# Stick-breaking heads: additions to GpSimd, key copies to ScalarE, and the keys' lo over all 128 rows

## The chip, the core and the metric

The kernel runs on one core of a Trainium2 chip. The time is device microseconds of one execution, the median of several runs; the profiled execution is a further one. TensorE multiplies matrices, VectorE and ScalarE work element by element, GpSimd does so too but only on SBUF, and SyncE issues most of the loads.

## The reference, cut to what matters

Two blocks are applied to 512 tokens of width 1024, all in float32: a first one with a convolution layer and a pooling layer, a second one with stick-breaking attention, retention and a feed-forward part. The change touches the stick-breaking attention alone, 16 heads of width 64:

```
for i in range(s_len // BLOCK):            # BLOCK = 128, four query blocks
    end = (i + 1) * BLOCK
    z = einsum('bhtd,bhsd->bhts', qb, kb) * scale          # scale = 64 ** -0.5
    mask = s_pos[None, :] < t_pos[:, None]
    log_1m_beta = where(mask, log_sigmoid(-z), 0.0)
    after = cumsum(log_1m_beta, axis=3, reverse=True) - log_1m_beta
    log_a = log_sigmoid(z) + after
    a = where(mask, exp(log_a), 0.0)
    outs.append(einsum('bhts,bhsd->bhtd', a, vb))
```

With s = softplus(z) = -log_sigmoid(-z), log_a is z minus the sum of s over this key and all later ones, up to the query. So the kernel needs, for each head, the scores, their softplus, sums of it from the end, one exponential and the product with v.

## The kernel before

Every float32 operand of a matmul is split into a coarse part "hi" and the rest "lo" (both float32r), and a product is three matmuls: hi by hi, hi by lo, lo by hi. The weights come in 244 groups of 128x1024. For each group ScalarE casts the hi (L294) and VectorE subtracts for the lo (L299), two groups ahead of their use.

**Layout of a head.** Scores are kept transposed: keys on the 128 rows, queries on the columns. For key block j only queries from j*128 on count, so four blocks of 512, 384, 256 and 128 columns are laid into three PSUM banks, numbered n: bank 0 has block 0 (512 columns), bank 1 blocks 1 and 3 (384 + 128), bank 2 block 2 (256). They are worked through in the order 1, 2, 0. Tiles of banks 0 and 1 are named "s" (512 wide), those of bank 2 "u" (256 wide). PSUM: banks 0 and 1 come from four "z" buffers, bank 2 from two "r" buffers. Projections and head outputs take turns in two "m" buffers.

**Queries and keys.** A projection gives two heads, one on rows 0 to 63, one on 64 to 127. The tile of a query (`sb_q`) holds its hi on the rows of its head and its lo on the other 64 rows. For a key (`sb_k`) ScalarE takes the two hi from PSUM (L1065), VectorE subtracts both lo into the two halves of one tile (L1068), and VectorE copies each hi to the other 64 rows as well (L1070). So one 128-row matmul of the doubled key hi with the query tile gives hi by hi and hi by lo at once (L1097), and a 64-row matmul adds lo by hi (L1106).

**Softplus** (L1113 to L1127): VectorE takes the minimum with 40 (L1113), ScalarE an exponential (L1114) and a logarithm (L1115), VectorE a maximum with z (L1118). Then the softplus of later key blocks is added: block 2 takes block 3 (128 columns), block 1 takes block 2 (256), block 0 takes block 1 (384), all on VectorE (L1124). The sums are split: VectorE casts hi (L1080), GpSimd subtracts lo (L1081). Six matmuls with a triangle of -1 (L1135) and six with its complement (L1138) add the sums to the scores in PSUM, first with the three hi, then with the three lo. ScalarE takes the exponential (L1144); it is split in the same way (L1080 or L1078, then L1081), and eight matmuls with v (L1159) give the output in an "m" buffer. L1165 and L1167 put its two halves together.

**Order.** In this stage (`tc.manual_schedule`) ScalarE, GpSimd, VectorE and TensorE run their instructions in the order in which the program writes them. Each head is one step of six acts, STEP = "WOSFFF". In step h, W is `sb_weights` of head h (L1135, L1138, L1144), O is `sb_out` of head h-1 (L1159 to L1167), S is `sb_scores` of head h+2, and each F is the next piece of other work: half of a projection to q or k (12 matmuls of 512 columns), or a quarter of a v projection (24 of 256). F's come in a cycle of four steps: step 4 has q4 and the first half of k4, step 5 the second half of k4 and then q5, step 6 k5 and a quarter of v2, step 7 the rest of v2; the same holds for steps 0 to 3 and 8 to 11. From step 12 on there are four F's and they belong to the retention part.

The work of the other engines is written later than what it follows: after each act comes a `tick`, and a task that yields a number goes on after so many ticks, older tasks first. WAIT holds these numbers. With 2 for "min" and 1 for "max", the minimum of head h+2 is written after the first F of step h, the maximum and the first two additions after the second. With 2 for "split", the casts and subtractions of banks 2 and 1 of a head, the maximum and the addition of its bank 0 come after W of the step before its own, and the split of its bank 0 after S of that step. `finish` writes whatever is left of a task at once. The exponential of head h is split after S of step h (WAIT 3).

Of the kernel before, what the change touches and what calls it, by code (L numbers as in the profile page):

```python
# [9 lines left out]
F32 = mybir.dt.float32  # L10
F32R = mybir.dt.float32r
AF = mybir.ActivationFunctionType
ALU = mybir.AluOpType

P = 128
T = 512
# [51 lines left out]
).split()  # L68

WAIT = {"v": 1, "q": 1, "k": 1, "min": 2, "max": 1, "split": 2, "exp": 3, "out": 0}  # L70
START = "FFSFFFSFFF"
STEP = "WOSFFF"
ON = {"sp": "VVV", "aa": "AVA"}
# [60 lines left out]
def body(ctx: ExitStack, tc, ap, out):  # L134
# [12 lines left out]
    def nm(p):  # L147
        uid[0] += 1
        return f"{p}{uid[0]}"
# [16 lines left out]
    def at(tag="a", dt=F32, n=T):  # L166
        return phase[0].pool[tag].tile([P, n], dt, tag=tag, name=nm(tag))
# [4 lines left out]
    def pm():  # L172
        return psm.tile([P, T], F32, tag="m", name=nm("m"))

    def pz():
        return at("z")
# [4 lines left out]
    def pr():  # L181
        return psr.tile([P, T], F32, tag="r", name=nm("r"))

    def f(x):
        return x.bitcast(F32)

    mm = nc.tensor.matmul
    V, A, G = nc.vector, nc.scalar, nc.gpsimd

    HALF = (slice(0, 64), slice(64, 128))  # L190
# [6 lines left out]
    with tc.high_priority(offset=20000):  # L197
        for k in range(KC):
            t = const.tile([P, T], F32, name=nm("x"))
# [103 lines left out]
    def block(i, n=1):  # L303

        g, r = divmod(at_block[0] + i, GB)
        hi, lo = group(g)
        return hi[:, r * P:(r + n) * P], lo[:, r * P:(r + n) * P]

    def mm3(o, l, r, first, last):
        mm(o, l[0], r[0], start=first, stop=False)  # L310
        mm(o, l[0], r[1], start=False, stop=False)  # L311
        mm(o, l[1], r[0], start=False, stop=last)  # L312
# [505 lines left out]
    with tc.manual_schedule(engines=HAND):  # L818
# [7 lines left out]
        for k in range(KC):  # L826
            t = at("c")
# [63 lines left out]
    for i in range(4):  # L891
        t = at("v" if i < 2 else "p")
# [74 lines left out]
    n2 = Norm(lambda k: geff[:, 16 + k:17 + k], lambda k: mod[:, 48 + k:49 + k], "c")  # L967
# [17 lines left out]

    q_, k_, v_, osb = {}, {}, {}, []

    def lin_in(m):

        o = pm()  # L990
        for k in range(KC):
            mm3(o, block(0), h[k], k == 0, k == KC - 1)
            at_block[0] += 1
            if k == KC // 2 - 1:
                yield
        return o
# [33 lines left out]
    def post(work):  # L1030
        tasks.append([0, work])
        run(tasks[-1])
        return work
# [7 lines left out]
    def finish(work):  # L1041
        for t in list(tasks):
            while t[1] is work and t in tasks:
                run(t)

    def split_steps(o, t):
        A.copy(out=t[:, :, 0, :], in_=o)
        yield WAIT["v"]
        V.tensor_sub(out=t[:, :, 1, :], in0=o, in1=f(t[:, :, 0, :]))

    def sb_q(i, o):

        q_[i] = [at("a", F32R) for _ in HALF]
        for t, a in zip(q_[i], HALF):
            A.mul(out=t[a], in_=o[a], mul=0.125)
        yield WAIT["q"]
        for t, a, b in zip(q_[i], HALF, HALF[::-1]):
            V.scalar_tensor_tensor(out=t[b], in0=o[a], scalar=0.125, in1=f(t[a]), op0=ALU.mult, op1=ALU.subtract)

    def sb_k(i, o):  # L1060

        res, lo = [at("a", F32R) for _ in HALF], at("a", F32R)
        k_[i] = res, lo
        for t, a in zip(res, HALF):
            A.copy(out=t[a], in_=o[a])  # L1065
        yield WAIT["k"]
        for t, a in zip(res, HALF):
            V.tensor_sub(out=lo[a], in0=o[a], in1=f(t[a]))  # L1068
        for t, a, b in zip(res, HALF, HALF[::-1]):
            V.tensor_copy(out=t[b], in_=f(t[a]))  # L1070

    def sb_tile(n, dt=F32):
        return at("u", dt, T // 2) if n == 2 else at("s", dt)

    def sb_split(t, n, w, on):
        hi, lo = sb_tile(n, F32R), sb_tile(n, F32R)
        if on[n] == "A":
            A.copy(out=hi[:, 0:w], in_=t[:, 0:w])  # L1078
        else:
            V.tensor_copy(out=hi[:, 0:w], in_=t[:, 0:w])  # L1080
        G.tensor_tensor(out=lo[:, 0:w], in0=t[:, 0:w], in1=f(hi[:, 0:w]), op=ALU.subtract)  # L1081
        return hi, lo

    def sb_scores(hd):
        i, r = hd // 2, HALF[hd % 2]
        finish(ready.pop(f"q{i}", None))
        finish(ready.pop(f"k{i}", None))
        q, kh, kl = q_[i][hd % 2], k_[i][0][hd % 2], k_[i][1]
        zs, sp = {}, {}
        for n in (1, 2, 0):  # L1090
            bank = BANKS[n]
            z = pz() if n < 2 else pr()
            w = bank[-1][1] + bank[-1][2]
            zs[n] = z, w
        of_block = [(zs[n][0][:, off:off + wj], j, bi) for n in (1, 2, 0) for bi, (j, off, wj) in enumerate(BANKS[n])]
        for o, j, bi in of_block:
            mm(o, kh[:, j * P:j * P + P], q[:, j * P:T], start=bi == 0, stop=False, skip_group_check=True)  # L1097
        for n, (z, _) in zs.items():
            if len(BANKS[n]) == 2:
                m2 = z.rearrange("p (a b) -> p a b", a=4)[:, 0:4:3, :]  # L1100
                mm(m2, identr, mask.unsqueeze(1).to_broadcast([P, 2, P]), start=False, stop=False, skip_group_check=True)
            else:
                mm(z[:, 0:P], identr, mask, start=False, stop=False, skip_group_check=True)

        for o, j, bi in of_block:
            mm(o, kl[r, j * P:j * P + P], q[r, j * P:T], start=False, stop=True, skip_group_check=True)  # L1106

        def softplus():

            ts = {n: sb_tile(n) for n in zs}  # L1110
            yield WAIT["min"]
            for n, (z, w) in zs.items():
                V.tensor_scalar(out=ts[n][:, 0:w], in0=z[:, 0:w], scalar1=40.0, scalar2=None, op0=ALU.min)  # L1113
                A.activation(out=ts[n][:, 0:w], in_=ts[n][:, 0:w], func=AF.Exp)  # L1114
                A.activation(out=ts[n][:, 0:w], in_=ts[n][:, 0:w], func=AF.Ln, bias=1.0)  # L1115
            yield WAIT["max"]
            for n, (z, w) in zs.items():
                V.tensor_tensor(out=ts[n][:, 0:w], in0=z[:, 0:w], in1=ts[n][:, 0:w], op=ALU.max)  # L1118
                if n == 1:
                    continue  # L1120
                for j in (2, 1) if n == 2 else (0,):
                    (n1, o1, w1), (n2, o2, w2) = WHERE[j], WHERE[j + 1]
                    t1 = ts[n1][:, o1 + P:o1 + w1]
                    V.tensor_tensor(out=t1, in0=t1, in1=ts[n2][:, o2:o2 + w2], op=ALU.add)  # L1124
                yield WAIT["split"]
                for n1 in (2, 1) if n == 2 else (0,):
                    sp[n1] = sb_split(ts[n1], n1, zs[n1][1], ON["sp"])  # L1127

        return zs, sp, post(softplus())
# [127 lines left out]
    def lin_tok():  # L1257

        os = [pz() if j < 2 else pm() for j in range(4)]
        for k in range(KC):  # L1260
            wh, wl = block(0, 4)
            at_block[0] += 4
            for j, o in enumerate(os):
                hh, hl = cols(h[k], j * P, j * P + P)
                mm(o, hh, wh, start=k == 0, stop=False)  # L1265
                mm(o, hh, wl, start=False, stop=False)  # L1266
                mm(o, hl, wh, start=False, stop=k == KC - 1)  # L1267
        return [split(o) for o in os]
# [23 lines left out]
    def ret_out(sc, v, sg, meanwhile):  # L1292
        sq = Stat(G)
        oo = []
        for e in range(4):
            o = pz()
            for j in range(4):
                vl = cols(v[j], e * P, e * P + P)
                mm(o[:, j * P:T], vl[0], sc[j][0], start=j == 0, stop=False)
                mm(o[:, j * P:T], vl[0], sc[j][1], start=False, stop=False)  # L1300
                mm(o[:, j * P:T], vl[1], sc[j][0], start=False, stop=j == 3)
            oo.append(at("s"))
            V.tensor_tensor(out=oo[e], in0=o, in1=sg[e], op=ALU.mult)
            q2 = at("s")
            A.activation(out=q2, in_=o, func=AF.Square)  # L1305
            sq.add(q2)
        rb = pr()
        next(meanwhile)
        for i, _ in enumerate(rsqrt_steps(pr(), [sq.acc], 512, 0, T, rb)):
            if i == 1:  # L1310
                next(meanwhile)
        res = []
        for t in oo:
            V.tensor_tensor(out=t, in0=t, in1=rb, op=ALU.mult)
            hi, lo = at("a", F32R), at("a", F32R)
            A.copy(out=hi, in_=t)
            (G if len(res) % 2 else V).tensor_tensor(out=lo, in0=t, in1=f(hi), op=ALU.subtract)
            res.append((hi, lo))
        for _ in meanwhile:
            pass  # L1320
        return res
# [46 lines left out]
    for hd in range(RET_HEADS):  # L1368
        q, k_ = ret_in.pop(hd)
        if hd == 0:  # L1370
            osb = [split_in(osb[i], into=(at("o" if i else "s", F32R), at("s", F32R))) for i in range(KC)]
        v = lin_tok()
# [8 lines left out]
        res = ret_out(sc, v, sg, pairwise(ret_qk(hd + 1)) if hd < RET_HEADS - 1 else ret_branches())  # L1381
# [56 lines left out]
    with tc.manual_schedule(engines=HAND):  # L1438
# [5 lines left out]
        for a in (0, T // 2):  # L1444
            b = a + T // 2
            o = acc()
# [99 lines left out]
```

## Time and profile before

| | |
|---|---|
| median of 3 runs | 1676.9 us (1675.87 to 1680.08) |
| profiled execution | 1677.49 us, span 1675.7 us |
| TensorE busy | 1595.4 us (95%) |
| VectorE busy | 1015.4 us (61%) |
| ScalarE busy | 601.3 us (36%) |
| GpSimd busy | 498.4 us (30%) |
| granted TensorE clock, mean | 0.984 |

A matmul's duration in the trace overlaps that of the next, so TensorE's busy share is no measure of its speed. The stick-breaking stage runs from about 487 to 752 us of the span. A row of the timeline gives the start, the duration (of several instructions together where it ends in x2 or more), the engine (PE is TensorE, PEld its weight loads, DVE VectorE, ACT ScalarE, POOL GpSimd), the line, the tiles written and read, and in brackets how long the engine stood idle before and what ended that.

### The profile page before, as it was taken

The page shows a single profiled execution, that of the slowest core. Times are in us where ns is not written, and L with a number is a line of the kernel's source. Part 1 is how long each engine was busy: PE and PEld are TensorE (multiplying, and loading weights), DVE is VectorE, ACT ScalarE, POOL GpSimd, SP SyncE. Part 2 cuts the span into 40 slices and gives each one's busy share as a digit, 9 for nine tenths or more (in the row PEclk, how much of TensorE's full clock was granted, in tenths as well). Part 3 has the DMA queues.
Part 4 walks back from the last instruction along what each step waited for, and adds up shares of the span by engine and source line. Part 5 has one row for each costly group of instructions (what it writes and reads, how often), then busy time and mean ns, then how long its engine had stood idle before and what let it go on. Part 6 is the DMA issues. An engine that isn't in the chain of part 4 may idle for free.

```text
span 1675.7 us, 20285 instructions
## 1 busy us (share of the span) xinstructions
PE 1595.4 (95%) x7904; PEld 1345.8 (80%) x7904; DVE 1015.4 (61%) x1426; ACT 601.3 (36%) x896; POOL 498.4 (30%) x361
## 2 busy tenths in 40 slices
PE   6899899999989999999999999999999999999997
PEld 4688787877888888878878888888888888888887
DVE  6899978576678888886476644633254533333222
ACT  3434443433356566532332222223333522222221
POOL 2757854560124545550120201204431100000001
PEclk9999999899989999999999999999999999999999
DMA  7654544245621111215546232322232332332221
GB/s 253 200 187 158 178 139 145 89 146 183 223 75 52 56 59 51 76 64 172 170 149 210 96 115 66 104 88 76 90 99 76 101 100 91 99 101 93 96 91 61
DMA packets 59187, 195.91 MB, mean 117 GB/s; under 512 B 6609, under 2 KB 8913, under 8 KB 59090
## 3 DMA queue, kind: packets, MB, share of 16 engines
q1 hardware_dynamic: 57106, 191.46, 35.6%
q10 hardware_dynamic: 1984, 3.15, 0.6%
q8 instruction: 62, 1.02, 0.3%
q14 instruction: 35, 0.29, 0.1%
HBM read 192.48 MB, written 2.10 MB: 116 GB/s over the span
## 4 chain that ended last, share of the span: by engine, by line
PE 72%; DVE 13%; ACT 6%; issue 4%; DMA 3%; POOL 2%; SPq 0%; POOLq 0%; DVEq 0%; ACTq 0%
PE m L310 10%; PE m L311 10%; PE m L312 10%; PE z L312 8%; PE z L310 8%; PE z L311 8%; DVE wlo L299 3%; DMA gw<-in_wmod 2%; DVE gw L255 2%; ACT whi L294 1%; DVE d L591 1%; PE z L1265 1%; PE m L1267 1%; PE m L1265 1%; PE z L1266 1%
## 5 line engine op out<-in xcount | busy, mean ns | idle before, releaser
L299 DVE TENSOR_TENSOR wlo<-w,whi 128x1024 fp32r<-128x1024 f32 (+1 forms) x243 | 333.0, 1373 | 376.8 <-ACT whi L294 375.8
L294 ACT CAST whi<-w 128x1024 fp32r<-128x1024 f32 x244 | 254.9, 1049 | 589.0 <-PE m L311 249.8
L310 PE MATMUL m<-h,whi 128*128 128x512 f32 x730 | 288.1, 395 | 4.0 <-ACT whi L294 1.5
L311 PE MATMUL m<-h,whi 128*128 128x512 f32 x730 | 285.7, 391 | 1.9 <-POOL h L483 1.9
L312 PE MATMUL m<-h,wlo 128*128 128x512 f32 x730 | 286.1, 392 | 1.3 <-DVE wlo L299 1.3
L310 PEld LDWEIGHTS m<-h,whi 128*128 128x128 f32 x730 | 137.7, 189 | 35.6 <-issue 2.0
L312 PEld LDWEIGHTS m<-h,wlo 128*128 128x128 f32 x730 | 137.7, 189 | 31.0 <-DVE wlo L299 2.2
L311 PEld LDWEIGHTS m<-h,whi 128*128 128x128 f32 x730 | 137.8, 189 | 29.6 <-POOL h L483 2.2
L310 PE MATMUL z<-h,whi 128*128 128x512 f32 x338 | 134.5, 398 | 5.3 <-ACT whi L294 5.3
L312 PE MATMUL z<-h,wlo 128*128 128x512 f32 x338 | 134.2, 397 | 0.9 <-DVE wlo L299 0.9
L311 PE MATMUL z<-h,whi 128*128 128x512 f32 x338 | 133.9, 396 | 0.0
L400 POOL TENSOR_TENSOR c<-c,c 128x512 f32<-128x512 f32 x10 | 13.3, 1334 | 374.4 <-ACT c L438 374.3
L400 POOL TENSOR_TENSOR s<-s,s 128x512 f32<-128x512 f32 x14 | 18.7, 1337 | 321.0 <-ACT s L1305 292.2
L1081 POOL TENSOR_TENSOR s<-s,s 128x512 fp32r<-128x512 f32 x64 | 92.8, 1459 | 30.7 <-DVE s L1080 30.7
L255 DVE CUSTOM_DVE_ANT_0 gw<-gw,cb,vec 128x1024 f32<-128x1024 f32 x64 | 93.7, 1469 | 8.1 <-DMA gw<-in_wmod 8.0
L312 PE MATMUL z<-a,wlo 128*128 128x512 f32 (+1 forms) x222 | 81.8, 368 | 1.5 <-DVE wlo L299 1.5
L310 PE MATMUL z<-a,whi 128*128 128x512 f32 (+1 forms) x222 | 82.2, 370 | 0.0
L311 PE MATMUL z<-a,whi 128*128 128x512 f32 (+1 forms) x222 | 81.5, 367 | 0.0
L310 PEld LDWEIGHTS z<-h,whi 128*128 128x128 f32 x338 | 65.1, 193 | 19.3 <-ACT whi L294 5.9
L312 PEld LDWEIGHTS z<-h,wlo 128*128 128x128 f32 x338 | 64.9, 192 | 15.8 <-DVE wlo L299 2.1
L311 PEld LDWEIGHTS z<-h,whi 128*128 128x128 f32 x338 | 64.9, 192 | 13.3
L310 PE MATMUL m<-a,whi 128*128 128x512 f32 (+1 forms) x196 | 72.3, 369 | 0.0
(418 smaller groups left out, 3501.9 us busy)
## 6 DMA issues: line engine op xcount, KB each, us to landing
w<-in_weights SPq DMA_DIRECT2D x244, 512.0 KB, 3.7
gw<-in_wmod SPq DMA_DIRECT2D x96, 512.0 KB, 4.3
a<-in_diag SPq DMA_DIRECT2D x32, 256.0 KB, 4.9
x<-in_xt SPq DMA_DIRECT2D x8, 256.0 KB, 5.0
s<-in_dec ACTq DMA_DIRECT2D x4, 256.0 KB, 3.5
out_x<-h SPq DMA_DIRECT2D x4, 256.0 KB, 2.5
p<-in_cnt ACTq DMA_DIRECT2D x2, 256.0 KB, 3.1
v<-in_cnt ACTq DMA_DIRECT2D x2, 256.0 KB, 3.4
```

The costliest lines, as they stand in the source:

```text
L255: product = V.tensor_tensor_reduce(out=t, in0=t, in1=cb[-1], scale=1.0, scalar=bias_of(j), op0=ALU.mult, op1=ALU.add, accum_out=mod[:, j:j ...
L294: A.copy(out=hi, in_=w)
L299: e.tensor_tensor(out=lo[:, part], in0=w[:, part], in1=f(hi[:, part]), op=ALU.subtract)
L310: mm(o, l[0], r[0], start=first, stop=False)
L311: mm(o, l[0], r[1], start=False, stop=False)
L312: mm(o, l[1], r[0], start=False, stop=last)
L400: self.eng.tensor_tensor(out=n, in0=self.acc, in1=t, op=ALU.add)
L591: V.scalar_tensor_tensor(out=cv[i], in0=y[:, j:j + T], scalar=tap(i, j), in1=cv[i], op0=ALU.mult, op1=ALU.add)
L1081: G.tensor_tensor(out=lo[:, 0:w], in0=t[:, 0:w], in1=f(hi[:, 0:w]), op=ALU.subtract)
L1265: mm(o, hh, wh, start=k == 0, stop=False)
L1266: mm(o, hh, wl, start=False, stop=False)
L1267: mm(o, hl, wh, start=False, stop=k == KC - 1)
```

## The change

Four edits, all in the stick-breaking stage. The three additions of L1124 are made by GpSimd instead of VectorE. The two copies of a key's hi to the other rows are made by ScalarE instead of VectorE. The lo of each of the two keys gets a tile of its own whose other 64 rows are zero, and the lo matmuls run over all 128 rows (the query's lo meets zeros). These tiles, three pairs in turn, lie in the six "g" buffers, which later hold the rotary tables and gates; GpSimd zeroes them once, with one memset and 12 copies, at the start of the stage. WAIT["split"] goes from 2 to 3.

```diff
--- before.py
+++ after.py
@@ -67,7 +67,7 @@
     "z7G z6G y5GAG m z4V g m y4GVV g m y7GAV m g y6VVG g m m g"
 ).split()
 
-WAIT = {"v": 1, "q": 1, "k": 1, "min": 2, "max": 1, "split": 2, "exp": 3, "out": 0}
+WAIT = {"v": 1, "q": 1, "k": 1, "min": 2, "max": 1, "split": 3, "exp": 3, "out": 0}
 START = "FFSFFFSFFF"
 STEP = "WOSFFF"
 ON = {"sp": "VVV", "aa": "AVA"}
@@ -985,6 +985,14 @@
 
     q_, k_, v_, osb = {}, {}, {}, []
 
+    klo = [[at("g", F32R) for _ in HALF] for _ in range(3)]
+    zeros = at("u", F32, T // 2)
+    G.memset(zeros, 0.0)
+    for lo in klo:
+        for t, b in zip(lo, HALF[::-1]):
+            for c in range(2):
+                G.tensor_copy(out=t[b, c * T // 2:(c + 1) * T // 2], in_=zeros[b])
+
     def lin_in(m):
 
         o = pm()
@@ -1059,15 +1067,15 @@
 
     def sb_k(i, o):
 
-        res, lo = [at("a", F32R) for _ in HALF], at("a", F32R)
-        k_[i] = res, lo
+        res, los = [at("a", F32R) for _ in HALF], klo[i % 3]
+        k_[i] = res, los
         for t, a in zip(res, HALF):
             A.copy(out=t[a], in_=o[a])
         yield WAIT["k"]
-        for t, a in zip(res, HALF):
+        for t, lo, a in zip(res, los, HALF):
             V.tensor_sub(out=lo[a], in0=o[a], in1=f(t[a]))
         for t, a, b in zip(res, HALF, HALF[::-1]):
-            V.tensor_copy(out=t[b], in_=f(t[a]))
+            A.copy(out=t[b], in_=f(t[a]))
 
     def sb_tile(n, dt=F32):
         return at("u", dt, T // 2) if n == 2 else at("s", dt)
@@ -1082,10 +1090,10 @@
         return hi, lo
 
     def sb_scores(hd):
-        i, r = hd // 2, HALF[hd % 2]
+        i = hd // 2
         finish(ready.pop(f"q{i}", None))
         finish(ready.pop(f"k{i}", None))
-        q, kh, kl = q_[i][hd % 2], k_[i][0][hd % 2], k_[i][1]
+        q, kh, kl = q_[i][hd % 2], k_[i][0][hd % 2], k_[i][1][hd % 2]
         zs, sp = {}, {}
         for n in (1, 2, 0):
             bank = BANKS[n]
@@ -1101,9 +1109,8 @@
                 mm(m2, identr, mask.unsqueeze(1).to_broadcast([P, 2, P]), start=False, stop=False, skip_group_check=True)
             else:
                 mm(z[:, 0:P], identr, mask, start=False, stop=False, skip_group_check=True)
-
         for o, j, bi in of_block:
-            mm(o, kl[r, j * P:j * P + P], q[r, j * P:T], start=False, stop=True, skip_group_check=True)
+            mm(o, kl[:, j * P:j * P + P], q[:, j * P:T], start=False, stop=True, skip_group_check=True)
 
         def softplus():
 
@@ -1121,7 +1128,7 @@
                 for j in (2, 1) if n == 2 else (0,):
                     (n1, o1, w1), (n2, o2, w2) = WHERE[j], WHERE[j + 1]
                     t1 = ts[n1][:, o1 + P:o1 + w1]
-                    V.tensor_tensor(out=t1, in0=t1, in1=ts[n2][:, o2:o2 + w2], op=ALU.add)
+                    G.tensor_tensor(out=t1, in0=t1, in1=ts[n2][:, o2:o2 + w2], op=ALU.add)
                 yield WAIT["split"]
                 for n1 in (2, 1) if n == 2 else (0,):
                     sp[n1] = sb_split(ts[n1], n1, zs[n1][1], ON["sp"])
```

## Rows read from the trace of the kernel before

**Rows 1.** Busy time by windows: stretch, length, then busy (instructions) per engine, clock, DMA, GB/s.
```profile
487.00:752.00 265.00, 252.35 (x1412) 219.00 (x1411) 225.81 (x345) 149.21 (x272) 126.73 (x101) 0.99 0.20 62
...
560.00:580.00 20.00, 19.05 (x124) 17.86 (x125) 16.15 (x30) 11.01 (x24) 8.85 (x9) 0.91 0.09 27
```

**Rows 2.** Waits of TensorE in the stage: total us, times, longest.
```profile
PE m L1159 <- DVE a L1068: 6.8, 3, 2.3
PE m L1159 <- DVE a L1058: 2.4, 3, 1.1
PE m L310 <- DVE o L1167: 0.9, 1, 0.9
```

**Rows 3.** Timeline of three engines, the first W and steps 2 to 3.
```profile
516.27 0.39 PE L1135 MATMUL z<-s,cstr 128*128 128x512 f32 x1
516.53 0.42 DVE L1049 TENSOR_TENSOR a<-m,a 128x256 fp32r<-128x256 f32 x1 [0.91 <-ACT a L1047]
...
546.42 0.58 ACT L1165 COPY o<-m 64x512 f32<-64x512 f32 x1
...
554.36 0.69 DVE L1113 TENSOR_SCALAR s<-z 128x512 f32<-128x512 f32 x1
...
560.95 1.83 PE L1159 MATMUL m<-s,a 128*128 128x512 f32 x4 [2.26 <-DVE a L1068]
```

**Rows 4.** Timeline of VectorE in step 4 and TensorE's output in step 5.
```profile
578.48 0.69 DVE L1167 TENSOR_TENSOR o<-m,o 64x512 f32<-64x512 f32 x1 [0.23 <-ACT o L1165]
...
584.47 0.69 DVE L1113 TENSOR_SCALAR s<-z 128x512 f32<-128x512 f32 x1
...
591.09 1.06 PE L1159 MATMUL m<-s,a 128*128 128x512 f32 x4 [1.13 <-DVE a L1058]
```

**Rows 5.** Timeline of GpSimd and VectorE in step 4.
```profile
579.77 3.58 POOL L1081 TENSOR_TENSOR s<-s,s 128x512 fp32r<-128x512 f32 x2 [1.94 <-DVE s L1080]
...
580.38 4.06 DVE L299 TENSOR_TENSOR wlo<-w,whi 128x1024 fp32r<-128x1024 f32 x2 [0.41 <-ACT whi L294]
```

**Rows 6.** GpSimd's subtractions L1081 by tile: ns min/median/max, first and last start.
```profile
L1081 POOL TENSOR_TENSOR s<-s,s x64: 1263/1298/2454, 509.3 to 745.8; 128x512 fp32r<-128x512 f32 x64
L1081 POOL TENSOR_TENSOR u<-u,u x32: 732/787/1719, 508.5 to 744.6; 128x256 fp32r<-128x256 f32 x32
```

**Rows 7.** Timeline of ScalarE, VectorE and TensorE in step 5.
```profile
597.35 1.17 ACT L1065 CAST a<-m 64x512 fp32r<-64x512 f32 x2 [3.34 <-PE m L312]
...
601.69 1.03 ACT L294 CAST whi<-w 128x1024 fp32r<-128x1024 f32 x1
...
602.58 0.39 PE L1135 MATMUL z<-s,cstr 128*128 128x512 f32 x1
...
602.75 1.23 DVE L299 TENSOR_TENSOR wlo<-w,whi 128x1024 fp32r<-128x1024 f32 x1 [1.40 <-ACT whi L294]
```

**Rows 8.** VectorE's additions L1124 by tile.
```profile
L1124 DVE TENSOR_TENSOR s<-s,u x16: 424/425/426, 502.7 to 722.1; 128x256 f32<-128x256 f32 x16
L1124 DVE TENSOR_TENSOR s<-s,s x16: 1484/1614/1632, 509.4 to 730.1; 128x384 f32<-128x384 f32 x16
```

**Rows 9.** Timeline of TensorE in the scores of step 5.
```profile
592.40 0.45 PE L1097 MATMUL z<-a,a 128*128 128x384 f32 x2
...
593.09 0.28 PE L1101 MATMUL z<-cstr 128*128 128x256 f32 x1
...
593.27 0.27 PE L1103 MATMUL z<-cstr 128*128 128x128 f32 x1
593.47 0.50 PE L1106 MATMUL z<-a,a 64*128 64x384 f32 x2
...
594.31 0.50 PE L310 MATMUL m<-h,whi 128*128 128x512 f32 x1
```

**Rows 10.** Timeline of GpSimd, its last instruction before the stage.
```profile
487.17 0.73 POOL L483 TENSOR_TENSOR h<-c,h 128x256 fp32r<-128x256 f32 x1 [0.78 <-ACT c L480]
```

**Rows 11.** ScalarE's casts from SBUF, L1078.
```profile
L1078 ACT CAST s<-s x16: 614/617/641, 519.4 to 742.3; 128x512 fp32r<-128x512 f32 x16
```

## The prediction

> **What bounds the kernel now.** The profiled execution took 1677.5 us (span 1675.7 us), 0.6 us above the median of the three runs, 1676.9. The sum below is made against 1677.5. About 5 us either way (0.3%) can't be told from no change, so "the same" is 1672 to 1682.
>
> I first took the busy time of the stick-breaking stage by windows [rows 1]. TensorE is busy 252 of 265 us there and VectorE 226: TensorE sets the pace, and VectorE has little room. Then I asked for what TensorE waited [rows 2]. Nearly all is one place: the output matmuls of L1159 wait, six times, 9.2 us in all, for VectorE's L1068 (lo of a key) or L1058 (lo of a query). That is a wait for a PSUM buffer: the output takes the "m" bank from which VectorE still subtracts. The reader should see that VectorE isn't slow on that instruction; it came to it late. The three longest of these waits follow steps 2, 6 and 10, the next steps 4 and 8. In the first of them VectorE started the `min` of head 4 at 554.36 and TensorE got the bank at 560.95, 6.6 us later [rows 3]. Between lie, in ScalarE's order, the exponentials and logarithms (3.3 us), the two ScalarE copies of the key and then VectorE's subtractions. So what ends last is when VectorE reaches the `min`. In step 4 it reached it at 584.47 and the bank came at 591.09, 6.6 us again [rows 4].
>
> Why VectorE is late there: its instructions with two SBUF inputs and GpSimd's take turns. In step 4 two GpSimd subtractions took 3.58 us [rows 5] where one takes 1.30 [rows 6], and two weight subtractions of VectorE 4.06 us [rows 5] where one alone takes 1.23 [rows 7]. Each waits for the other's whole instruction, alternately. The 384-column addition shows the same: 1.61 us, where 256 columns take 0.43 [rows 8].
>
> **The change part by part.**
>
> *Lo of the keys over 128 rows.* In step 5 the four full-height score matmuls take 0.69 us from the first start to the start of what follows (592.40 to 593.09). The four 64-row ones should start at about 593.33, 0.06 us after the last mask matmul, and the next 128-row matmul starts at 594.31: 0.98 us [rows 9]. If they run as the full-height ones do, 0.29 us a head is gained, 16 times: -4.6 us. Bounds: 0, if something else than the height costs it, and -5.6 us (0.35 a head, at the tightest spacing that the mask matmuls show). I take -4.6, since the same columns on the same engine just before are the nearest row.
>
> The Trainium skill, TensorE: Matmul & The Clock Gate, section LDWEIGHTS, says that a load's time hangs on its columns and not on its rows; by it alone this edit gives 0. No row here shows what a load waits for when the height changes.
>
> *Zeroing six tiles on GpSimd.* One memset and 12 copies of 64x256. No row shows such a copy; the nearest is GpSimd's 128x256 subtraction, 0.79 us [rows 6], so at most 13 x 0.79 = 10 us, at least half. GpSimd ends its last work of the stage before at 487.9 and has a first split only at 508.5 [rows 6, 10], so these 5 to 10 us lie in idle time. The first tile's copies must be done by 495, the first lo matmul: memset and four copies are 4.0 us at most. 0 us; without the cover it would be a few us once.
>
> *Three additions from VectorE to GpSimd.* From 1.30 us for 512 and 0.79 for 256 columns [rows 6] GpSimd should need 0.5, 0.8 and 1.0 us for 128, 256 and 384: 2.3 us a head. VectorE is freed of about as much. But the two take turns, so the time in which either holds the shared path hardly falls, and an instruction of VectorE that needs a sum now waits for GpSimd. The Trainium skill, GPSIMD Engine Reference, section Engine selection, says that elementwise work belongs on VectorE and takes about twice as long on GpSimd: the rule that speaks against this edit. Rival C is its price, worked out from rows.
>
> *Copies of the keys' hi on ScalarE.* Two a key, 64x512, SBUF to SBUF. ScalarE's own SBUF cast of 128x512 takes 0.62 us [rows 11] and its copy from PSUM 0.58 [rows 7]: 1.2 us a key. VectorE is freed of two casts.
>
> *WAIT["split"] from 2 to 3.* It counts ticks, and it is used twice for a head. The casts of the first two banks move from behind W to behind O; the cast of bank 0 moves from behind S to behind the second F. Only one F is left between that cast and the W that needs it. Here new waits arise:
>
> 1. Steps 1, 5 and 9, where a key's projection ends in the first F. In step 5 ScalarE takes the key from PSUM at 597.35 and then does exponentials and logarithms; the next weight cast L294 starts at 601.69, VectorE's L299 behind it at 602.75, and W starts at 602.58 [rows 7]. After the change the two ScalarE copies stand between the logarithms and L294, so L294 is at 602.9 and L299 ends at 605.2. The cast of bank 0 is behind L299 on VectorE (second F), so it ends at 605.6. W needs it in its third matmul, 0.35 us after 602.58: a wait of 2.7 us that was not there. Bank 0's lo (GpSimd, 1.3 us) then comes 0.1 to 0.4 us late for the second part. 2.8 us, three times: +8.4 us. If the copies were free, 1.6 each, +4.8.
>
> 2. The first head: its bank 0 is split only when W forces it, behind L1049 that ends at 516.95. The cast ends at 517.35, and the matmul that needs it ran at 516.27 [rows 3]: 1.1, and 0.4 for the lo: +1.5 us.
>
> 3. Steps 4 and 8. VectorE, until now busy with casts behind W, is idle until L1167 at 578.48 [rows 4], then does two casts, a max, a third cast (which waits for GpSimd's 1.3 us) and two L299s, which alternate with GpSimd's addition and subtraction. From the end of L1167 at 579.2 I add 0.3 + 0.4 + 0.7 to 580.6, wait to 581.6, cast 0.3, addition 0.9, L299 1.1, subtraction 1.1, L299 1.1: `min` at 586.1; if the cast slips in before a subtraction, 585.1. Now it is 584.47. So the wait for the bank grows by 0.6 to 1.6 us, 1.1 on average, twice: +2.2 us. Should the turns fall the other way, it could be -2.6 (both present waits gone).
>
> 4. Steps 2, 6 and 10. Only one L299 is left before the `min`. From L1165 at 546.42 [rows 3] the same addition gives L1167 to 547.7, casts and max to 549.0, GpSimd's subtraction to 550.1, cast, addition, L299: 552.5, 1.9 us before the present 554.36. But the two ScalarE copies then stand in front of the weight cast and of the exps (L1144), whose banks the next scores reuse: about 0.75 us is given back. -1.1 us, three times: -3.3 us. Bounds: -7.3 (waits gone) and 0.
>
> 5. After the longest wait the granted clock was 0.91 in 560 to 580 us [rows 1], up to 1.8 us. As new waits of the same length come, I take half: -0.9 us. The late L1167 [rows 2] becomes earlier, since additions and casts no longer stand before it: -1.0 us, once.
>
> Sum: -4.6 + 8.4 + 1.5 + 2.2 - 3.3 - 0.9 - 1.0 = +2.3 us: 1679.8, say 1680 us.
>
> **The rivals.** *A. The same, 1680 us:* gains and new waits cancel. Its own range is 1672 to 1682. Chance 0.38.
>
> *B. Faster, about 1668 us.* VectorE's relief counts for more: the waits of [rows 2] go (-9.2), the rows give -4.6, the clock -1.8, and of item 1 only +4.8, with +1.5: -9.3. For it: all present waits come from VectorE's lateness, and it gives up 2.3 us a head. Against: item 1 needs no contention at all, only the order of ScalarE and VectorE. Chance 0.25; it decides once item 1 costs less than about 1.5 us a step.
>
> *C. Slower, about 1689 us.* GpSimd becomes the chain: from the output's end ScalarE's copy 0.6, L1167 0.7, cast 0.3, then seven GpSimd instructions, 0.8 + 1.3 + 1.0 + 1.3 + 0.7 + 1.3 + 1.3, to bank 0's lo: 9.3 us, against 11.3 us from 592.6 until W's second part wants it, 1.3 us after W's start at 602.58. Each L299 in between adds 1.1. With two of them and three casts, 12.4: a wait of 1 us in 9 of 12 heads turns +2.3 into +11. For it: the turns in [rows 5]. Against: in eight of twelve steps at most one L299 falls there. It decides from 0.3 us a head on. Chance 0.37, in which I count 0.1 for the case that the 64-row edit gives nothing (0 instead of -4.6: 1684 us).
>
> **How the numbers follow.** 1680 us is that of A. The range takes in B's 1668 and C with a little of the other bound, 1691: outside lie about one in ten on either side. Faster by over 0.3%: 0.25, within: 0.38, slower: 0.37.
>
> **What would show it.** The four lo matmuls should be 128 rows and 0.63 to 0.69 us long. In steps 1, 5 and 9 the matmul L1135 of bank 0 should wait for VectorE's cast L1080, by 2.5 to 3 us. L1159's waits should shrink to about 1 us in steps 2, 6 and 10. If GpSimd's L1081 leads the list of what TensorE waits for, it is C. If TensorE waits for no cast L1080 at all, item 1 is wrong and with it the forecast. GpSimd's additions should show 0.5 to 1 us; 2 us each would mean that turns cost them what they cost VectorE's.

## The result and the profile after

The changed kernel took 1688.61 us (median of 4 runs, 1686.94 to 1690.72) against 1676.38 for the kernel before on the same chip: ratio 1.0064, 95% interval 1.0041 to 1.0088. It is slower, by 0.64%. The forecast of 1680 was 9 us too low; the time lies inside the range, where rival C was put. The profiled execution took 1690.19 us (span 1688.3), 12.7 us more than that of before. One execution of the kernel before, in the first set of the experiments, took 2231.7 us and is left out of every ratio and mean clock below. All lines from L995 on have moved by 7 or 8: W is now L1142 and L1145, the cast L1088, GpSimd's subtraction L1089, the output L1166, the additions L1131, the lo matmuls L1113.

The windows view of the whole stage answers to the first line of [rows 1].

```profile
487.00:752.00 265.00, 245.35 (x1353) 213.65 (x1351) 182.11 (x268) 153.17 (x278) 165.93 (x159) 0.97 0.18 58
```

VectorE is relieved as intended: 182 us busy instead of 226. GpSimd rose from 127 to 166. TensorE did less in the same time, and its granted clock fell from 0.99 to 0.97. So the engine that looked full was emptied by a fifth and the kernel became slower. The list of what TensorE waits for in the stage (total us, times, longest), its first six lines, says why; it answers to [rows 2]:

```profile
PE z L1142 <- DVE s L1088: 9.6, 6, 2.7
PE m L1166 <- DVE a L1066: 4.0, 2, 2.0
PE m L310 <- DVE s L1192: 2.1, 1, 2.1
PE m L1166 <- DVE g L1076: 1.6, 3, 0.7
PE z L1105 <- ACT s L1151: 1.0, 4, 0.5
PE z L1142 <- POOL s L1089: 0.9, 5, 0.2
```

The output's wait for a key's lo (now a "g" tile) shrank from 6.8 to 1.6 us. At the top stands one that was not there: W waits for the cast of its bank 0. Before the scores (L1105) TensorE now waits in four places for ScalarE's L1151, where the kernel before has one such wait, of 0.5 us. GpSimd's L1089 holds W up for 0.9 us in all. The timeline of ScalarE, VectorE and TensorE in step 5 answers to [rows 7]:

```profile
603.29 1.25 ACT L1078 CAST a<-a 64x512 fp32r<-64x512 f32 x2
604.57 1.04 ACT L294 CAST whi<-w 128x1024 fp32r<-128x1024 f32 x1
...
605.64 1.23 DVE L299 TENSOR_TENSOR wlo<-w,whi 128x1024 fp32r<-128x1024 f32 x1 [4.21 <-ACT whi L294]
606.79 0.42 DVE L1088 CAST s<-s 128x512 fp32r<-128x512 f32 x1
...
604.31 0.28 PE L1142 MATMUL r<-u,cstr 128*128 128x256 f32 x1
607.26 0.50 PE L1142 MATMUL z<-s,cstr 128*128 128x512 f32 x1 [2.67 <-DVE s L1088]
...
608.69 0.79 PE L1142 MATMUL z<-s,cstr 128*128 128x512 f32 x1 [0.17 <-POOL s L1089]
```

The reader should see VectorE idle for 4.21 us, not busy: it stands at L299, which wants the hi that ScalarE casts behind the two copies, and the 0.4 us cast that TensorE needs is queued behind L299. Steps 1 and 9 show the same 2.67.

The timeline of step 4 and the start of step 5 answers to [rows 4]; below it, the windows view of steps 5 and 6, from W to W.

```profile
577.15 0.69 DVE L1174 TENSOR_TENSOR o<-m,o 64x512 f32<-64x512 f32 x1 [3.02 <-ACT o L1172]
...
584.75 0.68 DVE L1120 TENSOR_SCALAR s<-z 128x512 f32<-128x512 f32 x1
...
587.02 0.50 PE L1142 MATMUL z<-s,cstr 128*128 128x512 f32 x1 [0.35 <-DVE s L1088]
...
588.46 0.50 PE L1142 MATMUL z<-s,cstr 128*128 128x512 f32 x1 [0.18 <-POOL s L1089]
...
591.36 1.83 PE L1166 MATMUL m<-s,a 128*128 128x512 f32 x4 [2.00 <-DVE a L1066]
```
```profile
586.17:604.08 17.91, 15.39 (x68) 12.70 (x67) 9.46 (x17) 12.44 (x24) 9.47 (x10) 0.90 0.15 55
604.08:622.05 17.97, 15.12 (x80) 13.13 (x79) 12.49 (x18) 9.51 (x17) 10.50 (x10) 0.91 0.18 59
```

After its 2.00 us of waiting the output's four matmuls take 1.83 us; after the 1.13 us of [rows 4] they took 1.06. That is the clock: right after the wait TensorE runs at 1.2 GHz for a while, and then at 2.4 again. The mean of such a step is 0.90 or 0.91, so it loses (1 - 0.905) x 18 = 1.7 us. Five stretches of this kind lie in the stage: in these two steps, in their counterparts 9 and 10, and in step 14. In the kernel before it was one, the line of 0.91 in [rows 1]. Not every wait has one behind it: the W that ends step 1 waits 2.67 us as well, and from its start to the next W the clock is full.

```profile
541.37:557.99 16.62, 13.77 (x81) 11.87 (x80) 12.48 (x18) 9.52 (x17) 10.52 (x10) 1.00 0.20 64
```

The scores of a head whose steps hold no wait answer to [rows 9]:

```profile
576.30 0.45 PE L1105 MATMUL z<-a,a 128*128 128x384 f32 x2
...
577.16 0.27 PE L1111 MATMUL z<-cstr 128*128 128x128 f32 x1
577.27 0.45 PE L1113 MATMUL z<-a,g 128*128 128x384 f32 x2
...
577.96 0.40 PE L310 MATMUL m<-h,whi 128*128 128x512 f32 x1
```

The four lo matmuls take 0.69 us to the start of L310. And the steps without any wait (W to W) went from 13.41 to 13.07 us, from 16.13 to 15.79: 0.34 us a head are gained.

Last, GpSimd's new work: the additions by tile, and its zero copies, which lie in idle time as predicted.

```profile
L1131 POOL TENSOR_TENSOR u<-u,s x16: 448/460/474, 501.6 to 734.3; 128x128 f32<-128x128 f32 x16
L1131 POOL TENSOR_TENSOR s<-s,u x16: 727/738/1665, 502.1 to 734.8; 128x256 f32<-128x256 f32 x16
L1131 POOL TENSOR_TENSOR s<-s,s x16: 1008/1192/2324, 509.7 to 744.3; 128x384 f32<-128x384 f32 x16
...
487.59 4.72 POOL L994 CAST g<-u 64x256 fp32r<-64x256 f32 x12
```

### The profile page after: what moved, and what is told of

Read it like the earlier page. It is cut to its first block, busy times and chain, and to the rows that moved or that the text cites. A ratio compares the mean times of both kernels' runs of the same rounds, so it can differ in the third digit from the quotient of the medians.

```text
span 1688.3 us, 20257 instructions
## 1 busy us (share of the span) xinstructions
PE 1600.9 (95%) x7904; PEld 1350.6 (80%) x7904; DVE 981.9 (58%) x1362; ACT 610.7 (36%) x912; POOL 543.0 (32%) x422
## 4 chain that ended last, share of the span: by engine, by line
PE 72%; DVE 12%; ACT 6%; issue 4%; POOL 3%; DMA 2%; SPq 0%; POOLq 0%; DVEq 0%; ACTq 0%
PE m L310 10%; PE m L311 10%; PE m L312 10%; PE z L312 8%; PE z L310 8%; PE z L311 8%; DVE wlo L299 3%; DVE gw L255 2%; ACT whi L294 1%; DMA gw<-in_wmod 1%; DVE d L591 1%; PE z L1273 1%; PE m L1274 1%; PE m L1273 1%; PE z L1272 1%
## 5 line engine op out<-in xcount | busy, mean ns | idle before, releaser
L299 DVE TENSOR_TENSOR wlo<-w,whi 128x1024 fp32r<-128x1024 f32 (+1 forms) x243 | 333.1, 1374 | 392.3 <-ACT whi L294 391.3
L294 ACT CAST whi<-w 128x1024 fp32r<-128x1024 f32 x244 | 254.9, 1049 | 594.7 <-PE m L311 257.3
L310 PE MATMUL m<-h,whi 128*128 128x512 f32 x730 | 287.5, 394 | 5.2 <-DVE s L1192 2.1
L310 PEld LDWEIGHTS m<-h,whi 128*128 128x128 f32 x730 | 138.0, 189 | 33.8 <-ACT u L1086 2.2
L310 PE MATMUL z<-h,whi 128*128 128x512 f32 x338 | 133.8, 396 | 5.4 <-ACT whi L294 5.4
L400 POOL TENSOR_TENSOR c<-c,c 128x512 f32<-128x512 f32 x10 | 13.3, 1335 | 374.0 <-ACT c L438 373.8
L1089 POOL TENSOR_TENSOR s<-s,s 128x512 fp32r<-128x512 f32 x64 | 94.4, 1479 | 25.1 <-DVE s L1088 24.3
L310 PE MATMUL z<-a,whi 128*128 128x512 f32 (+1 forms) x222 | 82.1, 370 | 0.0
L310 PEld LDWEIGHTS z<-h,whi 128*128 128x128 f32 x338 | 64.4, 190 | 19.2 <-ACT whi L294 6.1
L310 PE MATMUL m<-a,whi 128*128 128x512 f32 (+1 forms) x196 | 72.3, 369 | 0.0
```

What stands on the lines that cost most here:

```text
L294: A.copy(out=hi, in_=w)
L299: e.tensor_tensor(out=lo[:, part], in0=w[:, part], in1=f(hi[:, part]), op=ALU.subtract)
L400: self.eng.tensor_tensor(out=n, in0=self.acc, in1=t, op=ALU.add)
```

## The experiments

Ratios are to the kernel before on the same chip (its medians there were 1677.87, 1679.19 and 1676.79 us in the three sets).

**Rows alone.** The kernel before with only the lo tiles of 128 rows and their zeros.

```diff
+    klo = [[at("g", F32R) for _ in HALF] for _ in range(3)]
...
-            mm(o, kl[r, j * P:j * P + P], q[r, j * P:T], start=False, stop=True, skip_group_check=True)
+            mm(o, kl[:, j * P:j * P + P], q[:, j * P:T], start=False, stop=True, skip_group_check=True)
```

> The kernel before with the lo of the keys over 128 rows alone (six zeroed tiles); additions and key copies stay on VectorE, split at 2. Order theory (the edits cost through the order in which casts are written, the rows edit is a gain of its own): steps 4, 8, 12 and 13 got 0.31 to 0.34 us shorter in the changed kernel without any wait in them, so 16 x 0.34 = 5.4 us are gained: 1671 us. Rival, the rows give nothing and those steps are shorter for VectorE's relief: 1676 us.

Measured: 1677.65 us, ratio 1.0004 (0.9983 to 1.0025). My figure was wrong, the rival's right. The steps without waits are 13.07 long here too, so the 0.34 us are there. A part of them is given back at the output, as its list of waits shows (its profiled run took 1685.04 us, 7 more than the median, so I read waits from it and no total):

```profile
PE m L1166 <- DVE g L1076: 7.9, 3, 2.7
PE m L1166 <- DVE a L1066: 3.5, 3, 1.5
```

With the 6.8 and 2.4 of [rows 2] that is 2.2 us more. In these six steps TensorE arrives earlier, and VectorE, which frees the bank, does not. In the others the 0.34 us stay. Where the remaining 3 us go isn't shown; the mean granted clock of the 12 runs is 0.981, that of the kernel before in this set 0.983, which would be 3 us, but single runs of either lie anywhere from 0.977 to 0.989.

**The three suspects one by one, taken out of the changed kernel.** Copies two ticks later, WAIT back to 2, additions back on VectorE:

```diff
         for t, lo, a in zip(res, los, HALF):
             V.tensor_sub(out=lo[a], in0=o[a], in1=f(t[a]))
+        yield 2
         for t, a, b in zip(res, HALF, HALF[::-1]):
             A.copy(out=t[b], in_=f(t[a]))
```

> The changed kernel, with ScalarE's two key copies written two ticks later, so that the weight cast comes first on ScalarE. Order theory: the wait of W for the cast of bank 0 in steps 1, 5 and 9 falls from 2.84 to about 1.6 us, 3.7 us in all: 1685 us, and 1681 us if the stretches at 1.2 GHz behind these waits go too. Rival, GpSimd's additions cost it (they and VectorE take turns): no change, 1688 to 1689 us.

```diff
-WAIT = {"v": 1, "q": 1, "k": 1, "min": 2, "max": 1, "split": 3, "exp": 3, "out": 0}
+WAIT = {"v": 1, "q": 1, "k": 1, "min": 2, "max": 1, "split": 2, "exp": 3, "out": 0}
```

> The changed kernel with the split wait at 2 again. Order theory: the cast of bank 0 stands before the weight subtraction again, the waits in steps 1, 5 and 9 go (8.5 us) and with them one or two stretches at 1.2 GHz (1.7 us each); in exchange VectorE waits 1 to 2 us a head for GpSimd's 384-column addition, which TensorE sees in part: 1677 us, 1673 to 1682. Rival, GpSimd's additions cost it: at least 1685 us.

```diff
-                    G.tensor_tensor(out=t1, in0=t1, in1=ts[n2][:, o2:o2 + w2], op=ALU.add)
+                    V.tensor_tensor(out=t1, in0=t1, in1=ts[n2][:, o2:o2 + w2], op=ALU.add)
```

> The changed kernel with the three additions on VectorE again, everything else as changed. Order theory: the waits of 2.8 us in steps 1, 5 and 9 need no GpSimd addition and stay; VectorE has 2.3 us a head more to do: 1688 to 1693 us. Rival, GpSimd's additions cost it: most of the 12 us comes back, 1675 to 1680 us.

| edit to the changed kernel | us | ratio | interval |
|---|---|---|---|
| copies later | 1678.23 | 0.9999 | 0.9983 to 1.0016 |
| WAIT 2 | 1676.85 | 1.0004 | 0.9990 to 1.0019 |
| additions on VectorE | 1688.09 | 1.0066 | 1.0047 to 1.0085 |

Two of the three results are in the range expected; with the copies later the kernel is 3 us faster than the better of the two figures of the order theory. Either change of order takes the whole slowdown away (with WAIT 2 the output's waits are back, 7.3 us for a key's lo and 4.1 for a query's, in place of W's); taking GpSimd's additions away changes nothing. With the additions on VectorE the first line of the list of waits is nearly the same as after, and that ends rival C as the cause:

```profile
PE z L1142 <- DVE s L1088: 8.9, 4, 2.7
```

With the copies later, the wait in steps 1, 5 and 9 falls by the copies' 1.25 us and a little more (list of waits):

```profile
PE z L1143 <- DVE s L1089: 5.4, 6, 1.3
```

By the lists that is about 3 us less waiting in all (between the starts of matmuls 5 us, 3 x 1.39 of them here), but 10 us less time. The rest is largely the clock. Windows of this kernel, the stage to step 4, step 5, and what follows; then the timeline of the output in steps 5 and 9:

```profile
486.00:582.00 96.00, 92.22 (x546) 81.39 (x546) 67.59 (x101) 61.43 (x110) 57.80 (x62) 1.00 0.20 62
582.00:600.00 18.00, 15.48 (x64) 12.83 (x63) 9.56 (x17) 11.19 (x23) 9.56 (x10) 0.81 0.17 57
600.00:752.00 152.00, 140.73 (x785) 121.80 (x784) 113.56 (x161) 85.25 (x156) 102.48 (x89) 1.00 0.20 63
```
```profile
587.28 1.83 PE L1167 MATMUL m<-s,a 128*128 128x512 f32 x4 [1.98 <-DVE a L1066]
...
649.22 1.05 PE L1167 MATMUL m<-s,a 128*128 128x512 f32 x4 [1.99 <-DVE a L1066]
```

Only step 5 is low; in it (1 - 0.81) x 18 = 3.4 us are lost, against 5 x 1.7 = 8.5 after: 5 us in this pair of profiles. Over all runs the mean granted clock is 0.984 here and 0.981 after, some 5 us too. Behind the shorter waits that end steps 1, 5 and 9 stands no slow stretch. The reader should also see what is not regular: the output waits equally long in steps 5 and 9, and only in step 5 does it go on at half speed.

**The wait number alone,** on the kernel before.

```diff
-WAIT = {"v": 1, "q": 1, "k": 1, "min": 2, "max": 1, "split": 2, "exp": 3, "out": 0}
+WAIT = {"v": 1, "q": 1, "k": 1, "min": 2, "max": 1, "split": 3, "exp": 3, "out": 0}
```

> The kernel before with one number changed, WAIT split 3 instead of 2. Order theory: the cast of bank 0 stands behind the last L299 of steps 1, 5 and 9 without any ScalarE copies, so TensorE waits for it about 1.6 us in each of the three (2.84 less the two copies' 1.25), +4.8 us, the first head adds about 1, and the output's waits of rows 2 shrink a little in steps 2, 6 and 10: 1680 us (1676 to 1685). Rival (the late cast matters only together with the copies): no wait for that cast in steps 1, 5 and 9, and 1676 us or less.

Measured: 1684.33 us, ratio 1.0044 (1.0027 to 1.0062), as the order theory said. The cast's wait is there without any copies; list of waits, and VectorE in step 5:

```profile
PE z L1135 <- DVE s L1080: 4.8, 4, 1.3
```
```profile
599.54 1.23 DVE L299 TENSOR_TENSOR wlo<-w,whi 128x1024 fp32r<-128x1024 f32 x1 [1.94 <-ACT whi L294]
600.68 0.42 DVE L1080 CAST s<-s 128x512 fp32r<-128x512 f32 x1
```

So WAIT 3 costs some 5 to 7 us by itself. The copies in ScalarE's queue double the wait of step 5 (1.3 to 2.67). The changed kernel with later copies has the shorter wait too and is none the slower for it, so there its other edits pay for WAIT 3; whether it is the rows or VectorE's relief wasn't tested.

**The minimum earlier,** to remove the output's waits at their root ("min" 1 and "max" 2): on the kernel before, with the rows, and on the changed kernel with later copies.

```diff
-WAIT = {"v": 1, "q": 1, "k": 1, "min": 2, "max": 1, "split": 2, "exp": 3, "out": 0}
+WAIT = {"v": 1, "q": 1, "k": 1, "min": 1, "max": 2, "split": 2, "exp": 3, "out": 0}
```

> The kernel before with the minimum of head h+2 written right after its scores, one tick earlier (WAIT min 1, max 2), so ahead of the weight subtractions. If what ends last before the output is when VectorE reaches the minimum, the output's waits of 9.2 us shrink to 3 or less and the kernel takes about 1670 us (1666 to 1673). Rival (VectorE has no room, so whatever is put first makes something else late): the waits reappear at another place, for instance for the weights' lo or the sums' hi, and the time stays at 1674 to 1680.

> The kernel before with the lo of the keys over 128 rows and the early minimum, no other edit. If the 0.34 us a step that the 128 rows save were swallowed by the output's wait for its bank, they show once that wait is gone: about 1664 us (1660 to 1668), some 5 below the early minimum alone. Rival (the rows' saving is swallowed by any wait that happens to be there): the same as the early minimum alone within 2 us.

> The changed kernel with ScalarE's key copies written two ticks later and the early minimum. If both places of waiting are orders of work, it loses the wait of steps 1, 5 and 9 and most of the output's waits: about 1667 us (1662 to 1672). Rival (the additions on GpSimd make the minimum late or the sums late whatever the order): no better than the changed kernel with later copies, 1675 to 1680.

Measured: 1696.43 (ratio 1.0107, 1.0086 to 1.0129), 1693.60 (1.0090, 1.0067 to 1.0113) and 1688.44 us (1.0064, 1.0039 to 1.0089). All three expectations of a gain were wrong. The output's waits for a lo did go, but the exponentials that follow the minimum now stand ahead of L294 on ScalarE. List of waits of the first of these kernels, then ScalarE and TensorE in step 2:

```profile
PE m L1008 <- ACT whi L294: 6.6, 3, 2.2
```
```profile
560.10 1.03 ACT L294 CAST whi<-w 128x1024 fp32r<-128x1024 f32 x1
...
561.18 0.38 PE L1008 MATMUL m<-whi,h 128*128 128x256 f32 x1 [2.19 <-ACT whi L294]
```

The rows add nothing on top: W of head 0 to W of head 15 takes 234.6 us with and without them.

**Bank 0 split early again,** the changed kernel with the casts of banks 1 and 2 behind O but that of bank 0 behind S; and the same with the copies later.

```diff
-                yield WAIT["split"]
+                yield WAIT["split"] if n == 2 else 1
```

> The changed kernel with the split of bank 0 written two ticks earlier, after S as in the kernel before; the casts of banks 1 and 2 stay behind O, and the ScalarE copies stay where they are. Order theory: the slowdown is the cast of bank 0 standing behind the last L299 before W. The waits for that cast (9.6 us in six places) go but for 1 us at the first head, the stretches of low clock that follow them too, and the time is about 1677 us (1672 to 1681). Rival (the ScalarE copies are themselves the cost, since they delay L294 and so the weights or the exponentials): waits for the weights' hi or lo appear in steps 1, 5 and 9, and 1683 us or more.

> Both mendings at once: the split of bank 0 after S and the ScalarE copies two ticks later. If each mends the same wait, the second adds nothing: about 1676 us (1671 to 1680), within 2 us of the earlier split alone. If the copies cost something besides, it is 3 us or more below the earlier split alone.

Measured: 1698.88 (ratio 1.0128, 1.0106 to 1.0150) and 1694.34 us (1.0095, 1.0073 to 1.0117). Half of the theory held: W no longer waits for that cast at all, and no weight is waited for longer than 0.4 us. But the output's waits are now twice those of [rows 2]. List of waits, and VectorE in step 4:

```profile
PE m L1166 <- DVE a L1066: 9.4, 3, 4.1
PE m L1166 <- DVE g L1076: 8.7, 3, 2.9
```
```profile
582.26 0.76 DVE L1088 CAST s<-s 128x512 fp32r<-128x512 f32 x2 [2.13 <-POOL s L1131]
...
587.40 0.68 DVE L1120 TENSOR_SCALAR s<-z 128x512 f32<-128x512 f32 x1
...
592.47 1.39 DVE L1066 SCALAR_TENSOR_TENSOR a<-m,a 64x512 fp32r<-64x512 f32 x2 [1.84 <-ACT a L1063]
```

Here the moved addition does cost: the cast of bank 0 waits 2.13 us for GpSimd's L1131, which comes behind two subtractions there, and everything behind the cast, the minimum included, waits with it. From L1174 to the minimum it is 9.35 us here, 7.60 after, 5.99 before [rows 4]. In the changed kernel the cast stood behind the minimum, so this cost was hidden. This is read from the rows; no run has the early cast with the additions on VectorE. With the copies later as well the time is 4.5 us less, though the two intervals touch, so the copies seem to cost something besides.

**The bank freed first,** on the kernel before, and as the third of three mendings on the changed one: the lo of a query or key subtracted right behind ScalarE's copy, and the minimum one tick later.

```diff
-WAIT = {"v": 1, "q": 1, "k": 1, "min": 2, "max": 1, "split": 2, "exp": 3, "out": 0}
+WAIT = {"v": 1, "q": 0, "k": 0, "min": 3, "max": 1, "split": 2, "exp": 3, "out": 0}
```

> The kernel before with the bank of a query or key freed first: its lo is subtracted right behind ScalarE's copy (WAIT q and k 0 instead of 1), and the minimum of head h+2 is written one tick later (WAIT min 3), so that ScalarE's exponentials stand behind that copy and not ahead of it. If the output's waits of 9.2 us are only the order of that work, they go, nothing else comes late since the sums are wanted a step later, and the time is about 1666 us (1662 to 1671). Rival (as with the early minimum, the work put later makes the weights' casts or the sums late): waits for the weights' hi or lo or for the sums' casts in their place, 1676 us or more.

> The changed kernel with the earlier split of bank 0, the later copies, and the bank of a query or key freed first. If the changed kernel's gains (0.34 us a step from the rows, less work on VectorE) were only swallowed by waits that the order makes, it beats all others: about 1662 us (1656 to 1668). Rival: some engine has no room left and the waits move, 1674 us or more.

Measured: 1730.89 (ratio 1.0311, 1.0286 to 1.0336) and 1719.04 us (1.0257, 1.0224 to 1.0290), far worse than either theory. The first kernel's output waits for no lo any more; the scores wait instead. List of waits, then ScalarE and TensorE in step 3:

```profile
PE z L1097 <- ACT s L1144: 24.7, 10, 3.3
```
```profile
577.38 0.63 ACT L1115 ACTIVATE s<-s 128x512 f32<-128x512 f32 x1
577.92 1.03 ACT L294 CAST whi<-w 128x1024 fp32r<-128x1024 f32 x1
...
579.24 0.60 ACT L1144 ACTIVATE s<-z 128x512 f32<-128x512 f32 x1
...
579.90 0.51 PE L1097 MATMUL z<-a,a 128*128 128x384 f32 x2 [3.31 <-ACT s L1144]
```

The scores reuse the bank that L1144 reads, and L1144 now stands behind the later exponentials and L294. I had not asked who waits for what stands behind the moved work on ScalarE. No kernel tried is measurably faster than the one before.

## Why the prediction was right and wrong

Each term of the sum, against what the two traces show. Both run the same matmuls in the same order, so a wait is measured here between the starts of the same two matmuls, before and after. The lists of waits show less, since they count idle time from the modelled end of the matmul before: the W that ends step 5 starts its third matmul 2.95 us after its second, usually 0.12, so the wait costs 2.83 us and not 2.67.

| step | predicted | measured | from |
|---|---|---|---|
| lo over 128 rows | -4.6 | -5.4 | 16 x 0.34 |
| 1: steps 1, 5, 9 | +8.4 | +9.5 | 3 x (2.83 + 0.33) |
| 2: first head | +1.5 | +1.3 | two gaps between starts of 1.19 and 0.40 us, usually 0.12 |
| 3: steps 4 and 8 | +2.2 | +3.4 | 2 x (0.86 at the output, 0.51 and 0.33 at W) |
| 4: steps 2, 6, 10 | -3.3 | -3.5 | 5.2 less at the output, 3 x 0.57 more at the scores |
| 5: clock | -0.9 | +6.8 | four more stretches of 1.7 |
| late L1167 | -1.0 | +1.2 | its 1.0 went, 2.2 for L1192 came |
| sum | +2.3 | +13.3 | of 12.7 |

**The step that failed is item 5.** It had the wrong sign and is 7.7 us off; all others together are 3.3 us too low (-0.8, +1.1, -0.2, +1.2, -0.2, +2.2). I halved the clock's loss of the stage "as new waits of the same length come", that is, I saw that new waits came and still booked a gain. In fact three waits of 2.3 us were exchanged for six of 2.0 to 2.7, and five slow stretches stood in place of one. With +6.8 there, the sum gives 1687.5, and case A would not have been the likeliest.

How much of this loss the waits bring isn't settled, since the clock differs from run to run. The +6.8 us are of one profile of each kernel. Over the whole kernel it is 5 us in these two profiles, as one slow stretch fewer lies ahead of the stage, and 4 to 6 us by the mean granted clock of all runs, 0.981 after (4 runs) and 0.983 to 0.984 for the kernel before in the three sets. But with WAIT 2, in a kernel as fast as the one before, the stage has 0.97 in its profile too:

```profile
487.00:752.00 265.00, 250.51 (x1401) 220.46 (x1400) 177.43 (x275) 157.45 (x286) 166.83 (x162) 0.97 0.19 61
```

That shorter waits bring back the clock is supported by the kernel with later copies, against this one; that each single stretch comes from the wait ahead of it is not shown, since equal waits had none behind them.

From W of head 0 to W of head 15 the stage took 222.2 us before and takes 237.0 after, 14.8 more. The table has 14.0 of them, since the lo of two heads lies ahead. Ahead of that first W 2.3 us were gained; among it are the lo of these two heads and a wait of 0.8 us for VectorE's L1049 that is gone.

**Item 1** was right in mechanism and nearly in size, in all three steps: 3.2 us each, 2.8 predicted. The copies account for about half of each wait and WAIT 3 for the rest. **Item 3** came out at the upper of its two ends: 7.6 us from L1174 to the minimum, where 6.6 or 7.6 were worked out. What I missed is that W itself waits there too, 0.84 us a step. **Item 4** came out as the difference that it was worked out as: VectorE's relief shortens the output's waits by 1.6 to 2.0 us a step, and the scores' waits for L1151, which stands behind ScalarE's copies, take 0.57 back (with the copies later these waits are gone).

**Late L1167.** Its wait went, but at the end of the stage one for L1192 came. GpSimd's 384-column addition took 2.32 us there, and behind it the cast, the minimum and L1192 came late (timeline of three engines):

```profile
726.70 2.32 POOL L1131 TENSOR_TENSOR s<-s,s 128x384 f32<-128x384 f32 x1
...
729.05 1.50 DVE L1088 CAST s<-s 128x512 fp32r<-128x512 f32 x1 [0.91 <-POOL s L1131]
...
738.03 0.68 PE L310 MATMUL m<-h,whi 128*128 128x512 f32 x1 [2.08 <-DVE s L1192]
```

The addition explains a part of this wait at most: with the additions on VectorE 1.4 us of it stay, and with WAIT 2 and the additions on GpSimd it is 0.5. So it is mainly WAIT 3 that makes L1192 late.

**The rows.** The size was right (0.29 a head predicted, 0.34 measured), the worth was not: alone the edit is worth 0 within 0.25%. Of the 5.4 us 2.2 go to longer waits for the output's bank, which VectorE frees; for the rest the clock is a candidate, not shown. I had not made a free bank a condition of the -4.6. The Trainium skill, TensorE: Matmul & The Clock Gate, section LDWEIGHTS, says that a load's time doesn't hang on its rows. The trace agrees as to the load itself (medians of 184 and 186 ns for 64 rows, 188 and 192 for 128); the time is lost where the height changes.

**Rival C** had the right time for the wrong reason. GpSimd's L1089 held W up for 0.9 us where 9 were priced, and with the additions on VectorE the time is the same. **Rival B** failed where it said it would: item 1 cost 3.2 us a step, not 1.5. The Trainium skill, GPSIMD Engine Reference, section Engine selection, would keep elementwise work on VectorE. The trace agrees on the single instruction (0.46 and 0.74 us against 0.29 and 0.42, 1.6 to 1.7 times); no price on the kernel's time shows in this order of work, and a wait of 2.1 us in step 4 shows once the cast of bank 0 stands ahead of the minimum.

## What to carry to other kernels

Where engines work in a fixed order, a busy share doesn't say what relief is worth: VectorE lost a fifth of its work here and the kernel slowed down, because a 0.4 us cast was queued behind an instruction that waited for another engine's queue. For each moved instruction, ask on its new engine and its old one what stands behind it and who waits for that; seven kernels here that moved work to repair one wait made another, at L294, at the minimum or at L1144, and none of them beat the kernel before. And price a new wait of TensorE with the clock that may follow it: here 1.7 us on top, behind five of six waits of 2.0 to 2.7 us.

## What was not expected of the hardware

Going from 128-row to 64-row matmuls and back costs about 0.34 us each time a head does it, although the load is no slower (184 and 186 ns against 188 and 192): the start of the first 64-row matmul comes 0.20 us after the last 128x128 one (0.11 with 128 rows), the second 0.28 us after the first (0.23), the first 128-row matmul 0.32 us after the last 64-row one (0.23), and the next after that 0.33 us later (0.23).

In the changed kernel each slow stretch took 1.7 us from its step and began within 2 us of TensorE's restart after a wait of 2.0 us or more. But one of its three waits of 2.67 us had none behind it, and in the kernel with later copies the same wait of 2.0 us had one in one step and none in the other, so it could be priced on average only.
